# A two-layer encoder on one core: other slots for attention's sums and retention's keys, and one product issued in two pieces

## The chip, the cores and the metric

One core of a Trainium2 chip runs the whole program. The metric is the device time of one execution in microseconds (us). TensorE (PE) multiplies, VectorE (DVE), ScalarE (ACT) and GpSimd (POOL) work on elements, and SyncE (SP) issues nearly all transfers from one queue.

## The reference

Two sequences of 512 tokens, `x_prompt` and `x_sample`, go through the same two layers of width 1024. Below they are the two groups `g`. Each layer adds its mixer's output to `x`, after a norm of the rows of `x`; a last norm ends it. Both mixers have 8 heads, 256 wide.

```python
# layer 0: attention as a difference of two softmaxes per head
q, k, v, gate = split(h @ w_in)                  # 1024 -> 8192
p = softmax(rotary(q) @ rotary(k).T)             # 16 maps of 512 x 512, two per head
a = p[:, :, 0] - lam * p[:, :, 1]
o = rms_norm(a @ v) * silu(gate);  x = x + o @ w_out
# layer 1: retention in both directions
q, k, v, gate = split(h @ w_in)                  # 1024 -> 6144
scores = (q @ k.T) * intra;   o = scores @ v + (q * q_decay) @ state
state  = state * chunk_decay + (k * k_decay).T @ v
o = rms_norm(o_fwd + o_bwd) * silu(gate);  x = x + o @ w_out
```

## The kernel before

**Numbers in two parts.** Every matmul operand is kept as a high part and the rest that is left (`hi_of` on ACT, `lo_of` on DVE, both in fp32r). A product takes three matmuls, high by high, high by low, low by high (`PASSES`), which add up in one PSUM bank.

**Projections.** Both groups are projected together, with a scheme of seven products in place of eight. A `Unit` covers 256 output columns; its products are P1, P2, P5, P6, P3, P7 and P4 (`SEQ`). Each takes one operand made of weights, which lies in a ring of seven work buffers (`ws`), and four tiles made of activations: B11 in slots 0 to 3 (read by P1), B21 in 4 to 7 (P2), T1 in 8 to 11 (P5), T2 in 12 to 15 (P6), B22 in 16 to 19 (P3), T3 in 20 to 23 (P7), T4 in 24 to 27 (P4). A "pair" unit's product is 12 matmuls of 128x512 (`pair`, line 633; queries, keys and gates). A "wide" unit's is 48 of 128x256 (`wide`, line 643; the values): there the activations are stationary and the weights move. `product` issues a product, `evac` what follows it: P7's result is read from a bank (`sums`, line 687) to which P4 then adds. `projections` is a generator that yields after each product, so that the caller can lay other work between two of them. The P4 of a unit comes after the first product of the next; the last unit ends with P3, the P4 of the unit before it, P7, P4.

**Slots.** Most tiles lie in one arena, 18 x 1024 + 128 words of 4 bytes per partition, in slots 1024 words apart (slots 12, 13 and those from 20 on are tiles of their own; 14 to 19 follow 11 in the arena). A tile may be shifted by some words, and then reaches into the next slot's first words:

```python
lo = at * 1024 + shift
...
b.also = Buf(plan, f"edge{at + 1 if shift else at}", 1, None)
```

`edge` lets the plan know of it: a shifted tile must wait for the readers of the next slot too. Behind the arena lie the seven `ws` buffers of 1024 + 32 words with pads of 32 between them; values units use them from word 28 on.

**Heads of attention.** A step `i` of the loop is one tile of 128 queries of one head and group (64 steps). `scores` (line 1186) makes both maps' scores, 3 matmuls of 128x512 each; `row_max`, `exps` and `combine` make the difference of softmaxes; `transp` (line 1231) turns it; its high and low parts go to `aT`, slots 4 and 5, for two tiles together. `av` (line 1251) then multiplies: 24 matmuls of 128x256 for two tiles, values stationary, `aT` moving. `weighed` and `out_step` (lines 858 and 934) do the norm and the output projection. The last four products of the projections are laid between the first steps, one each in steps 0 to 3. Queries lie in slots 0 to 3 and keys in 6 to 9 (both unshifted), values in 10, 11, 14 and 15 shifted by 36.

**Heads of retention.** A block is one head of one group, done in two halves: `state2` (line 1409: keys turned, in slots 6 and 7 shifted by 36, times values, in 0 to 3 unshifted), `score2` (line 1385: keys stationary, queries moving, slots 4 and 5 shifted by 28), `av2` (line 1429: sums of the own half, values stationary and `aT` moving at a shift of 92; line 1437: those of the other half, queries moving). Blocks' tiles are loaded ahead by `fetch2`.

**Order.** Nothing is issued as it is written. All steps are recorded in a `Plan` with an estimated cost, what they read and what they write. `arrange` then plays them through with these estimates and writes out a fixed order for every engine and for SP's queue. PE's steps are taken in the order recorded, save that one that isn't ready lets up to 24 others pass. A product is one step to the plan, while on the chip a tile's next writer waits for the matmuls that read that tile.

Of the kernel before, what the change touches and what calls it, by code (L numbers as in the profile page):

```python
# [10 lines left out]
F32R = mybir.dt.float32r  # L11
# [4 lines left out]
P = 128  # L16
S = 512
D = 1024
KT = D // P
NT = S // P  # L20
# [235 lines left out]
def trunk_kernel(  # L256
# [8 lines left out]
    xs = (x_prompt, x_sample)  # L265
# [116 lines left out]
    def step(gen, n=1):  # L382
        for _ in range(n):
            next(gen, None)
# [24 lines left out]
    def pe(cost, fn, r, w, wait=0.0):  # L409
        plan.op("PE", cost, fn, r, w, wait=wait)  # L410
# [134 lines left out]
    class Unit:  # L545
# [71 lines left out]
            if op == "P2" and self.early is not None:  # L617
                self.early, self.x = None, {}

        def product(self, op):  # L620
            which = BANK_OF[op]
            n_banks = 2 if self.wide else 1
            opens = op in OPENS
            if opens:
                self.banks[which] = [bank(self.tags[which], which) for _ in range(n_banks)]
            a, b = self.ops.pop(op), B_OF[op]
            bt = [Bop[b, k] for k in range(4)]
            reads = [q[1] for q in a] + bt

            def pair(ps, ks=range(4)):  # L630
                for k in ks:
                    for i, (u, v) in enumerate(PASSES):
                        nc.tensor.matmul(  # L633
                            ps.t, a[u][0]()[:, k, :], bt[k][:, v, :], start=(opens and k == 0 and i == 0),
                            stop=(k == 3 and i == 2), skip_group_check=True)

            def wide(ps, t):
                if self.led and op == "P1" and t == 0:
                    for j in range(NT):
                        nc.tensor.transpose(ps[:, j * P:(j + 1) * P], ident.t, ident.t)  # L640
                for k in range(4):
                    for i, (u, v) in enumerate(PASSES):
                        nc.tensor.matmul(  # L643
                            ps[:, (t % 2) * 256:(t % 2) * 256 + 256], bt[k][:, v, t * P:(t + 1) * P],
                            a[u][0]()[:, k, :], start=(opens and t % 2 == 0 and k == 0 and i == 0),
                            stop=(k == 3 and i == 2), skip_group_check=True)

            if not self.wide:
                ps = self.banks[which][0]
                if op == "P1" and self in first_units[:2]:  # L650
                    def piece(k, half):
                        here = slice(half * 256, half * 256 + 256)
                        for i, (u, v) in enumerate(PASSES):
                            nc.tensor.matmul(
                                ps[:, here], a[u][0]()[:, k, :], bt[k][:, v, here], start=(half + k + i == 0),
                                stop=(k == 3 and i == 2), skip_group_check=True)
                    for half in range(2):
                        for k in range(4):
                            pe(0.36, lambda k=k, half=half: piece(k, half),
                               ([(a[0][1][0], (n, k)) for n in range(2)] if self is first_units[0] else reads[:2])  # L660
                               + [(bt[k], (0, half)), (bt[k], (1, half))], [(ps, (k, half))])
                else:
                    pe(2.79, lambda: pair(ps), reads, [ps])
                return
            for t in range(NT):
                ps = self.banks[which][t // 2]
                led = self.led and op == "P1" and t == 0
                pe(1.87 if led else 1.43, lambda ps=ps, t=t: wide(ps, t), reads + [ident] * led, [ps])
# [152 lines left out]
    def projections(units, early):  # L821

        n = 2 + len(early)
        for u, place in zip(units[2:], early):
            u.early = place
        order = product_order(units, n)
        ready = 0
        for n, (u, op) in enumerate(order):
            while ready < len(order):
                v, p = order[ready]  # L830
                if sum(w.n_ws for w, _ in order[n:ready]) + v.n_ws > WS_BUFS:
                    break
                v.prep(p)
                ready += 1
            u.product(op)
            u.evac(op)
            yield

# [33 lines left out]
    def load_qk(src, i, shift):  # L872
        t = slot(i, [P, 2, S], F32R, shift)
        dma(lambda: t.t.bitcast(F32), lambda: src[0][src[1]], [src[0]], [t], 512)
        return t
# [95 lines left out]
    qk_d = {}  # L971
# [194 lines left out]
    def fetch1(h, g, v=True):  # L1166
        for j in range(2):
            for which in range(2):
                qk[h, g, j, which] = load_qk((qk_d[0, which, h, g], j), 6 * which + 2 * g + j, 0)
        if v:  # L1170
            fetch1_v(h, g)

    def fetch1_v(h, g):
        vt[h, g] = load_v(v_d[0, h, g], 10 + 4 * g, 36)
        sg[h, g] = load_sg(g_d[0, h, g])

    def scores(i):
# [47 lines left out]
    def transp(i):  # L1225
        p, n = st[i]['p'], i % 2
        tp = bank("tp", "tpa")

        def fn():
            for j in range(NT):  # L1230
                nc.tensor.transpose(tp[:, j * P:(j + 1) * P], p[:, 0, j * P:(j + 1) * P], ident.t)  # L1231
        pe(0.44, fn, [p, ident], [tp])
        if n == 0:
            st[i]['aT'] = [slot(4 + u, [P, NT, 256]) for u in range(2)]
        aT, here = st[i - n]['aT'], slice(n * P, (n + 1) * P)
        src = lambda: tp.t.rearrange("p (j n) -> p j n", j=NT)
        hi_of(S, lambda: aT[0][:, :, here], src, [tp], [(aT[0], n)])
        lo_of(S, lambda: aT[1][:, :, here], src, lambda: aT[0][:, :, here], [tp, (aT[0], n)], [(aT[1], n)])
# [54 lines left out]
    for i in range(N + 5):  # L1293
        if i % 2 and i > 2:
            fill(1, LAG)
            at(av, i - 3, N)
        at(scores, i, N)
        at(row_max, i, N)
        at(exps, i, N)
        at(combine, i, N)  # L1300
        for n, when in enumerate((0, 1, 2, 3)):
            if i == when:
                step(proj, 1)
                if n >= 2:
                    new_xN(n - 2, lambda t, n=n: (xs[n - 2][0, t * P:(t + 1) * P, :], []))
                if n == 3:
                    fetch1_v(0, 1)
        if not i % 2 or i < 3:
            fill(1, LAG)
        at(transp, i - 1, N)  # L1310
        fill(1, LAG)
        if i % 2 == 0 and i > 3:
            at(weighed, i - 4, N)
        if i < N and i % 4 == 2 and i > 4:
            nh, ng = tiles[i][0:2]
            if ng == 1 and nh + 1 < NH:
                fetch1(nh + 1, 0)
            elif ng == 0 and nh > 0:
                fetch1(nh, 1)
# [24 lines left out]
    def fetch2(b):  # L1344
        h, g = blocks[b]
        for which in range(2):
            qk[b, which] = load_qk((qk_d[1, which, h - h % 2, g], h % 2), (4, 14)[which] + b % 2, (28, 128)[which])
        keys = len(plan.ops) - 1
        vt[b] = load_v(v_d[1, h, g], 2 * (b % 2), 0)
        t = kts[b] = slot(6 + b % 2, [P, 2, S], F32R, 36)  # L1350
        dma(lambda: t.t.bitcast(F32), lambda: kt_d[h, g].rearrange("a p c -> p a c"), [kt_d[h, g]], [t], 512)
        sg[b] = load_sg(g_d[1, h, g])
        return keys
# [22 lines left out]
    def score2(b, c):  # L1376

        h, g = blocks[b]
        s = bank("sc", "s2")
        q, k = qk[b, 0], qk[b, 1]  # L1380

        def fn():
            for j in range(2):
                for i, (u, v) in enumerate(PASSES):
                    nc.tensor.matmul(  # L1385
                        s[:, j * 256:(j + 1) * 256], k[:, u, (2 * c + j) * P:(2 * c + j + 1) * P],
                        q[:, v, c * 256:(c + 1) * 256], start=(j == 0 and i == 0), stop=(i == 2),
                        skip_group_check=True)
        pe(0.71, fn, [q, k], [s])
        t1 = e_t("rt")  # L1390
        F = Fs[h]
        dve(S, lambda: nc.vector.tensor_tensor(
            t1.t, s.t, F[:, 0:4, :].rearrange("p a b -> p (a b)"), op=ALU.mult),
            [s, *((F, n) for n in range(4))], [t1])
        aT = slot(8 + 2 * (b % 2) + c, [P, 2, S], F32R, 92)
        hi_of(S, lambda: aT[:, 0, :], lambda: t1.t, [t1], [(aT, 0)])
        lo_of(S, lambda: aT[:, 1, :], lambda: t1.t, lambda: aT[:, 0, :], [t1, (aT, 0)], [(aT, 1)])
        aTs[b, c] = aT
# [205 lines left out]
```

## Time and profile before

| | us |
|---|---|
| median of three runs (1807.0 to 1808.09) | 1807.33 |
| the profiled execution | 1806.59 |
| span of its instructions | 1804.5 |
| projections of layer 0, from the first to the last full stretch | 48 to 622 |
| attention, with the last four products at its start | 622 to 1010 |
| projections of layer 1 | 1055 to 1490 |
| retention | 1490 to 1804.5 |

Times within the execution are counted from the span's start. "PE o L1251 x24" in the chain of waits means 24 matmuls of line 1251 into a tile named `o`; L415, L419 and L422 are the helpers that record every transfer, high part and low part. In the busy time by stage, engines' columns hold busy us with the count of instructions, then TensorE's granted clock as a share of full speed, the mean busy share of the DMA engines, and GB/s.

### The profile page before, as it was taken

To read this page: it belongs to the slowest core of one execution; us is meant where nothing else is said; L and a number is where in the kernel's file an instruction comes from. 1 tells how busy PE (TensorE), PEld (TensorE's weight loads), DVE (VectorE), ACT (ScalarE), POOL (GpSimd) and SP (SyncE) were. 2 spreads that over 40 slices of the span, in tenths; PEclk is the share of its full clock that TensorE was granted. 3 is DMA by queue.
4 is the path that set the end of the run, shared out by engine and by line. 5 is a ranking of instruction groups with operands and counts; after the bars stand their busy time and mean duration, and the time that the engine had idled before them with its cause. 6 is when DMAs were issued, how large, how long until landed. Compare 5 with 4: busy or idle time off the path is not lost.

```text
span 1804.5 us, 27874 instructions
## 1 busy us (share of the span) xinstructions
PE 1789.8 (99%) x10333; PEld 1566.1 (87%) x10333; DVE 1479.1 (82%) x2344; ACT 895.9 (50%) x1865; POOL 169.2 (9%) x315
## 2 busy tenths in 40 slices
PE   9999999999999999999999999999999999999998
PEld 7889889898988888888888888898989998888887
DVE  8967878778699888888888897787887967888887
ACT  8753344443343565555454866444444455444446
POOL 1000000000000022322322200000000000111113
PEclk9999999999999999999999999999999999999999
DMA  6444455655545594444554524464647459664652
GB/s 218 134 134 135 158 150 166 199 164 155 177 124 187 204 344 179 172 162 156 179 205 140 195 68 147 140 210 156 207 151 231 144 182 399 262 232 185 228 216 94
DMA packets 162767, 328.81 MB, mean 182 GB/s; under 512 B 12724, under 2 KB 76872, under 8 KB 162632
## 3 DMA queue, kind: packets, MB, share of 16 engines
q1 hardware_dynamic: 162160, 326.18, 53.5%
q8 instruction: 81, 1.33, 0.3%
q10 hardware_dynamic: 472, 0.86, 0.1%
q14 instruction: 54, 0.44, 0.1%
HBM read 209.55 MB, written 117.44 MB: 181 GB/s over the span
## 4 chain that ended last, share of the span: by engine, by line
PE 93%; DVE 3%; ACT 1%; DMA 1%; issue 0%; POOL 0%; SPq 0%; ACTq 0%; POOLq 0%; DVEq 0%
PE pj L633 20%; PE pj L934 19%; PE sc L633 11%; PE pj L643 10%; PE o L633 8%; PE o L1251 5%; PE sc L643 5%; PE sc L1186 5%; PE o L1429 2%; PE o L643 2%; PE tp L1231 1%; PE sc L1385 1%; PE tp L1409 1%; PE o L1437 1%; DVE ws L422 1%; DMA raw<-in_da_w_out_dram 1%
## 5 line engine op out<-in xcount | busy, mean ns | idle before, releaser
L934 PE MATMUL pj<-ws,arena 128*128 128x512 f32 x1542 | 389.8, 396 | 0.0
L934 PEld LDWEIGHTS pj<-ws,arena 128*128 128x128 f32 x1542 | 277.3, 188 | 50.6
L633 PE MATMUL pj<-b,ws 128*128 128x512 f32 x1080 | 263.2, 390 | 0.0
L633 PEld LDWEIGHTS pj<-b,ws 128*128 128x128 f32 x1080 | 201.3, 188 | 41.7 <-DVE e L687 0.5
L939 DVE SCALAR_TENSOR_TENSOR b<-pj,pad,b 128x512 f32<-128x512 f32 (+1 forms) x257 | 190.2, 744 | 23.0 <-PE pj L934 21.7
L422 DVE TENSOR_TENSOR ws<-st,ws 128x512 fp32r<-128x512 f32 (+1 forms) x192 | 147.9, 774 | 70.4 <-ACT ws L419 52.8
L422 DVE TENSOR_TENSOR ws<-raw,ws 128x512 fp32r<-128x512 f32 (+2 forms) x167 | 141.9, 855 | 69.4 <-ACT ws L419 59.5
L419 ACT CAST ws<-st 128x512 fp32r<-128x512 f32 (+1 forms) x192 | 132.0, 693 | 123.4 <-PE pj L633 34.6
L633 PE MATMUL sc<-arena,ws 128*128 128x512 f32 x768 | 185.2, 390 | 0.0
L633 PE MATMUL o<-arena,ws 128*128 128x512 f32 x744 | 178.4, 391 | 1.1 <-DVE arena L482 1.1
L633 PEld LDWEIGHTS sc<-arena,ws 128*128 128x128 f32 x768 | 143.9, 188 | 29.7
L419 ACT CAST ws<-raw 128x512 fp32r<-128x512 f32 (+2 forms) x167 | 126.2, 762 | 84.7 <-PE o L633 46.6
L633 PEld LDWEIGHTS o<-arena,ws 128*128 128x128 f32 x744 | 138.5, 188 | 30.3 <-DVE arena L482 2.0
L633 PE MATMUL pj<-arena,ws 128*128 128x512 f32 x624 | 153.1, 390 | 0.0
L633 PEld LDWEIGHTS pj<-arena,ws 128*128 128x128 f32 x624 | 116.4, 188 | 23.9
L1204 ACT ACTIVATE b<-sc,pad 128x512 f32<-128x512 f32 x128 | 87.9, 688 | 69.3 <-DVE pad L1194 68.5
L679 ACT COPY c<-pj 128x512 f32<-128x512 f32 x104 | 60.9, 586 | 115.2 <-PE pj L633 62.7
L643 PE MATMUL pj<-ws,b 128*128 128x256 f32 x960 | 116.9, 275 | 0.0
L643 PEld LDWEIGHTS pj<-ws,b 128*128 128x128 f32 x960 | 113.3, 188 | 0.6
L1186 PE MATMUL sc<-arena 128*128 128x512 f32 x384 | 99.6, 393 | 0.0
L1251 PEld LDWEIGHTS o<-arena 128*128 128x128 f32 x768 | 96.1, 189 | 3.3 <-ACT arena L419 0.7
L1251 PE MATMUL o<-arena 128*128 128x256 f32 x768 | 97.1, 284 | 0.5 <-ACT arena L419 0.5
(221 smaller groups left out, 2875.9 us busy)
## 6 DMA issues: line engine op xcount, KB each, us to landing
qk<-os SPq DMA_DIRECT2D x192, 256.0 KB, 3.4
arena<-qk SPq DMA_DIRECT2D x96, 512.0 KB, 5.9
raw<-in_da_w_in_dram SPq DMA_DIRECT2D x64, 512.0 KB, 4.8
v<-os SPq DMA_DIRECT2D x64, 512.0 KB, 3.7
arena<-v SPq DMA_DIRECT2D x64, 512.0 KB, 4.2
raw<-in_ret_w_in_dram SPq DMA_DIRECT2D x48, 512.0 KB, 4.4
os<-g SPq DMA_DIRECT2D x32, 512.0 KB, 8.1
g<-e SPq DMA_DIRECT2D x48, 256.0 KB, 4.6
```

The lines of the kernel that those rows point to most:

```text
L419: act(n, lambda: nc.scalar.copy(dst(), src()), r, w)
L422: dve(n, lambda: nc.vector.tensor_tensor(dst(), src(), hi().bitcast(F32), op=ALU.subtract), r, w)
L633: nc.tensor.matmul(ps.t, a[u][0]()[:, k, :], bt[k][:, v, :], start=(opens and k == 0 and i == 0), stop=(k == 3 and i == 2), skip_group_che ...
L643: nc.tensor.matmul(ps[:, (t % 2) * 256:(t % 2) * 256 + 256], bt[k][:, v, t * P:(t + 1) * P], a[u][0]()[:, k, :], start=(opens and t % 2 == ...
L679: act(S, lambda c=c, ps=ps: nc.scalar.copy(c.t, ps.t), [ps], [c])
L934: nc.tensor.matmul(ps[:, here], o[a][:, e, t * P:(t + 1) * P], u[b][:, e, here], start=(m == 0), stop=(m == 5))
L939: axpy(n, lambda half=half, here=here, ps=ps: nc.vector.scalar_tensor_tensor(half, ps[:, here], rr[:, t % 2:t % 2 + 1], half, op0=ALU.mult ...
L1186: nc.tensor.matmul(s.t, q[:, a, t * P:(t + 1) * P], k[:, b, :], start=(n == 0), stop=(n == 2))
L1204: act(840, lambda j=j, s=s, m=m: nc.scalar.activation(p[:, j, :], s.t, AF.Exp, bias=m.t, accum_out=sm[:, 2 * j + n:2 * j + n + 1]), [s, m] ...
L1231: nc.tensor.transpose(tp[:, j * P:(j + 1) * P], p[:, 0, j * P:(j + 1) * P], ident.t)
L1251: nc.tensor.matmul(o[:, e * 256:(e + 1) * 256], v[b][:, j, e * P:(e + 1) * P], aT[a][:, j, :], start=(n == 0), stop=(n % 12 == 11), skip_g ...
L1429: nc.tensor.matmul(o[:, e * 256:(e + 1) * 256], v_[v][:, 2 * c + j, e * P:(e + 1) * P], a_[:, u, j * 256:(j + 1) * 256], start=(e == 0 and ...
```

## The change

Three things change, with what they bring along:

- In attention, `aT` is shifted by 28 words, the keys by 64 (`64 * which`; queries stay at 0), and the values by 64 where it was 36.
- In retention, the keys go from slots 14 and 15, shifted by 128, to slots 8 and 9, shifted by 64. The sums' tiles, which lay in slots 8 to 11, go to 10, 11, 14 and 15.
- The very last product of the first layer's projections is issued as two steps of six matmuls, with a yield between them; its bank is read after the second. The loop lays five pieces between its steps 0 to 4, and the second group's `x` is asked for in step 4 where it was step 3.

```diff
-        def product(self, op):
+        def product(self, op, part=None):
...
-            a, b = self.ops.pop(op), B_OF[op]
+            a, b = self.ops[op] if part == 0 else self.ops.pop(op), B_OF[op]
...
+                elif part is not None:
+                    ks = range(2 * part, 2 * part + 2)
+                    pe(1.4, lambda: pair(ps, ks), reads[:2] + [bt[k] for k in ks], [ps])
                 else:
                     pe(2.79, lambda: pair(ps), reads, [ps])
...
-            u.product(op)
+            if units is first_units and n == len(order) - 1:
+                u.product(op, 0)
+                yield
+                u.product(op, 1)
+            else:
+                u.product(op)
...
-                qk[h, g, j, which] = load_qk((qk_d[0, which, h, g], j), 6 * which + 2 * g + j, 0)
+                qk[h, g, j, which] = load_qk((qk_d[0, which, h, g], j), 6 * which + 2 * g + j, 64 * which)
...
-        vt[h, g] = load_v(v_d[0, h, g], 10 + 4 * g, 36)
+        vt[h, g] = load_v(v_d[0, h, g], 10 + 4 * g, 64)
...
-            st[i]['aT'] = [slot(4 + u, [P, NT, 256]) for u in range(2)]
+            st[i]['aT'] = [slot(4 + u, [P, NT, 256], F32R, 28) for u in range(2)]
...
-        for n, when in enumerate((0, 1, 2, 3)):
-            if i == when:
-                step(proj, 1)
-                if n >= 2:
-                    new_xN(n - 2, lambda t, n=n: (xs[n - 2][0, t * P:(t + 1) * P, :], []))
-                if n == 3:
-                    fetch1_v(0, 1)
+        if i < 5:
+            step(proj, 1)
+            if i in (2, 4):
+                new_xN(i // 2 - 1, lambda t, g=i // 2 - 1: (xs[g][0, t * P:(t + 1) * P, :], []))
+            if i == 3:
+                fetch1_v(0, 1)
...
-            qk[b, which] = load_qk((qk_d[1, which, h - h % 2, g], h % 2), (4, 14)[which] + b % 2, (28, 128)[which])
+            qk[b, which] = load_qk((qk_d[1, which, h - h % 2, g], h % 2), (4, 8)[which] + b % 2, (28, 64)[which])
...
-        aT = slot(8 + 2 * (b % 2) + c, [P, 2, S], F32R, 92)
+        aT = slot((10, 14)[b % 2] + c, [P, 2, S], F32R, 92)
```

## The prediction

> **What bounds the kernel now.** I read the page first, then busy time by stage, then the chain of waits in order of time; after that the groups by shape, the waits and the SP queue at the two places where a layer's projections give way to its heads.
>
> ```profile
> span 1804.5 us, 27874 instructions
> ```
>
> ```profile
> core 0: us, PE busy (x) PEld busy (x) DVE busy (x) ACT busy (x) POOL busy (x), PEclk, DMA share, GB/s
> 650.00:1010.00 360.00, 360.00 (x2063) 312.88 (x2062) 298.27 (x460) 187.06 (x503) 103.32 (x210) 1.00 0.49 178
> 1490.00:1516.00 26.00, 24.92 (x160) 22.30 (x160) 18.88 (x32) 15.90 (x31) 0.95 (x2) 1.00 1.03 399
> ```
>
> TensorE (PE) is the bound at a full granted clock. In attention (first stage row) it never idles, while VectorE (DVE) is busy 298.27 of 360 us, 83%. So a matmul that gets faster there shortens the run, until DVE's spare 17% is used up, which a gain of 1% does not do. Around the start of retention (second stage row) PE loses 1.08 us of 26, with the DMA engines full.
>
> "Busy" overlaps, so a matmul's true pace is read from the chain, where pieces follow each other without overlap:
>
> ```profile
> 440.33 5.48 PE pj L643 x48
> 445.81 2.75 PE pj L633 x12
> 448.56 5.48 PE o L643 x48
> 454.04 5.44 PE sc L643 x48
> ...
> 637.39 3.02 PE pj L633 x12
> 640.40 2.87 PE o L1251 x24
> 643.27 0.45 PE tp L1231 x4
> ...
> 646.50 3.14 PE o L1251 x24
> 649.64 1.38 PE sc L1186 x6
> ```
>
> ```profile
> L1251 PE MATMUL o<-arena 128*128 128x256 f32 x768 | 97.1, 284 | 0.5 <-ACT arena L419 0.5
> ...
> L643 PE MATMUL o<-ws,arena 128*128 128x256 f32 x384 | 45.1, 276 | 0.0
> ```
>
> Same engine, same shape (128x256, single column blocks, output in the same kind of bank): the values products (L643) take 5.44/48 = 113 ns each, the attention sums (L1251) 2.87/24 = 120 ns. The first 48 after a run of 512-column products take 5.48 instead of 5.44: a start that costs 0.04 us, and then the pace settles. L1251 starts anew 768/24 = 32 times.
>
> **Part 1: the places of the attention sums.** Counted in words and modulo 64 (slots lie 1024 apart, work buffers 1088 = 17 x 64 apart, and the arena is 290 x 64 long), the values products read their moving operand at 28 and their stationary one at 0; the attention sums read theirs at 0 and 36. The change puts them at 28 and 64, which is 28 and 0. Is it the place that makes 113? Retention has the same contrast:
>
> ```profile
> 1501.21 0.70 PE tp L1409 x6
> 1501.91 0.71 PE sc L1385 x6
> 1502.62 1.38 PE o L1429 x12
> 1504.00 0.68 PE o L1437 x6
> ```
>
> Its sums (L1429) read at 92 = 28 and 0: 12 in 1.38 us with the start included (115 ns), and the 6 of L1437 behind them, moving operand also at 28, take 113. Its state products (L1409) stand at 0 and 36, as attention does: 117, but only 6 long. So three lines agree with the place, and no row shows 0 and 36 settling. I take the pace of L643: 24 x 5.44/48 + 0.04 = 2.76 us a block for 2.87, 0.11 x 32 = 3.5 us. Leaving a settled block also costs: the 12 products behind one take 2.75 (at 445.81) where 12 in mid-stream take 2.72 (a settled run of 12, quoted in part 2), 0.03; the 6 scores behind an attention block take 1.38 where half of 2.72 is 1.36, 0.02 already paid. 0.01 x 32 = 0.3. **Net gain 3.2 us**; ends: 0 (place has no part in it) and 32 x (2.87 - 2.72) = 4.8 (no start cost). Nothing hides this: it is PE's own time on the chain.
>
> The Trainium skill, in the page SBUF — State Buffer, section "Who interferes with whom", speaks against this part: it gives PE two independent read ports, one for the moving operand and one for weights, and has PE wait for no one, so that addresses should not matter and this term would be 0. The trace does not quite agree: 113 and 120 ns stand side by side for one shape.
>
> Writing the sums at word 28 costs ACT and DVE nothing that a row shows: DVE's low halves into attention's slots (place 0) and retention's (place 28) take 684 and 682 ns.
>
> ```profile
> L422 DVE TENSOR_TENSOR arena<-tp,arena 128x512 fp32r<-128x512 f32 x64 | 43.8, 684 | 5.1 <-ACT arena L419 5.0
> ...
> L422 DVE TENSOR_TENSOR arena<-e,arena 128x512 fp32r<-128x512 f32 x36 | 24.4, 682 | 1.2 <-ACT arena L419 1.1
> ```
>
> The scores' keys go from 0 to 64, the same modulo 64: I take 0 for L1186. Its 384 products bound the error: by the nearest contrast of two paces at this width, 2.75 against 2.72 for 12, 0.0025 x 384 = 1 us either way.
>
> **Part 2: retention's keys in slots 8 and 9.** The chain at the start of retention:
>
> ```profile
> 1484.78 2.72 PE sc L633 x12
> 1487.50 2.73 PE pj L633 x12
> 1490.24 0.02 issue
> 1490.25 7.16 DMA arena<-qk
> ```
>
> ```profile
> PE sc L1385 <- DMA arena<-qk: 1.1, 1, 1.1
> ```
>
> The first score (L1385) waits for its keys, until 1490.25 + 7.16 = 1497.4. They go into slot 14 at +128, reaching into slot 15, which T2 holds until P6 ends; P6 is the 12 products from 1487.50, and the load leaves 0.02 after the end. In slots 8/9 at +64 it needs T1's first tiles, read by P5, which ends at 1487.50: up to 2.73 us earlier. With the same 7.16 it lands near 1494.7, while PE has work until 1497.4 - 1.1 = 1496.3. So **the 1.1 us go**, with 1.6 to spare. On SP the load passes two values loads and stores of the gate; the DMA engines are full there (1.03), and what it passes lands up to 0.5 MB / 399 GB/s = 1.3 us later. Nothing else in the stretch stops PE, so I take -1.1, with -1.2 and +0.2 (the wait merely changes its name) as ends. The sums' slots (10, 11, 14, 15 for 8 to 11) are filled by ACT when needed, after P5 and P6; no cost. Places modulo 64 stay, so no pace changes.
>
> **Part 3: the last product in two pieces, and attention's first keys.** The last P4 (12 matmuls, 2.72 settled) now comes as two sixes, one behind the scores of tile 3, one behind those of tile 4. It adds no matmul. From 637.39 to 646.50 PE's work is 2.72 + 2.87 + 0.45 + 1.38 (six scores) + 0.45 (four more transposes) + 0.22 (two more, half of four) = 8.1 of 9.1 us: 1.0 is lost, to these waits:
>
> ```profile
> PEld o L1251 <- ACT arena L419: 0.7, 1, 0.7
> ...
> PEld tp L1231 <- DVE arena L422: 0.5, 1, 0.5
> PEld pj L633 <- DVE e L687: 0.5, 1, 0.5
> ```
>
> The first six still wait for L687 (the sum of P7 reads the bank that P4 adds to). The sums of tiles 0 and 1 then start up to 1.4 us earlier, and the second six fill the wait for the transposes' bank. ACT's and DVE's chain to the next sums is late next. Against it stands a new wait: at +64 the second map's keys of head 0 (slot 7) reach into slot 8, T1 again, so their load waits for P5 where it waited for P2. PE order and SP order are both written out from the planner's estimates, which count P5 as a whole.
>
> ```profile
> 612.60 5.08 SPq L415 DMA_DIRECT2D arena<-qk  x4
> 620.08 0.32 SPq L415 DMA_DIRECT2D arena<-v  x1
> 620.45 0.90 SPq L415 DMA_DIRECT2D arena<-qk  x2
> ```
>
> ```profile
> DMA to landing us min/median/max: 3.2/5.5/10.1
> ```
>
> ```profile
> 622.61 1.52 PE L1186 MATMUL sc<-arena 128*128 128x512 f32 x6
> 623.97 2.88 PE L633 MATMUL o<-arena,ws 128*128 128x512 f32 x12
> ```
>
> Loads that P5 frees leave from 620.08. From there the keys land at 620.1 + 5.5 = 625.6, where the second scores of tile 0 ran at 622.61 + 0.68 = 623.3: 2.3 us late. P3 (2.72) can stand ahead of them and covers that; the tiles behind run some 2 us later, with four products of filler. I take -0.4 for the part; ends -1.0 (all of the lost time) and +2.3 (nothing covers the keys). Behind the waiting load on SP stand the other loads, the values and the second group's keys, which only later tiles read.
>
> **Sum.** The profiled execution took 1806.59 us (span 1804.5 and 2.1 around it), 0.74 below the median 1807.33. -3.2 - 1.1 - 0.4 = -4.7: 1801.9 for such an execution, **1802.6** beside the median. Two runs of this kernel are told apart from about 0.2%, 3.6 us.
>
> **Rivals.**
> A, *the place does nothing* and 120 is due to the order of reads within the block (the attention sums change their stationary tile per key block): for it, no row has the same instructions at two places; against it, L1429 has the same order at the other place and gets 115 with its start. Then -1.1 - 0.4 = -1.5: 1805.8. The port rule of the Trainium skill named above, in SBUF — State Buffer, would give this time.
> B, *another transfer takes the keys' place* in retention, since the engines move 399 GB/s there: for it, the share of 1.03; against it, the 1.6 to spare. Then -3.2 - 0.4 = -3.6: 1803.7.
> C, *attention's first scores wait*: the load of slot 7 leaves at 620.9, with the last of the three that P5 frees now, and takes the longest landing of the window, 10.1: 631.0 for 623.3, 7.7 us late. If P3 is not put ahead, all of it falls on PE: 7.7 + 0.4 - 4.7 = +3.4, 1810.7; with P3 ahead 5.0, +0.7, 1808.0. It ends slower than before once the scores start over 4.3 us late. For it: one SP queue, served in order, and landings of up to 10.1; against it: in the rows above four loads were taken one by one as tiles came free within a product, so this one could leave at about 618 (slot 8 is the first that P5 reads).
> D, *a new order elsewhere*: the planner lays the whole program out anew, and a misplaced step costs what the one at 1490 did, about 1 us each. The sum then lands 1 to 3 us higher, 1803.6 to 1805.6.
>
> **How the numbers follow.** Forecast 0.62, A 0.12, B 0.09, C 0.08, D 0.09. The forecast's own bounds, 32 blocks at 0.08 to 0.13 us and part 3 at -1.0 to +0.6, give 1801 to 1804. The range takes in B, A and most of D: 1800.8 to 1806.2, leaving C and odd ends out. Faster by over 0.2% means below 1803.7: 0.55 of the forecast's 0.62, half of B, a little of D: 0.62. Within 0.2%: the rest of these, A, and most of C: 0.31. Slower: 0.07, from C's far end and from what I don't see.
>
> **What would show it.** Right: in the chain, blocks of L1251 x24 at 2.74 to 2.78; its mean near 276 ns; no wait of L1385 for DMA, and the first score of retention 1 us or more closer to the product ahead of it; the stretch from the last P7 to the sums of tiles 2 and 3 shorter by some 0.4. Wrong: L1251 still at 2.87 (A); PE waiting for another transfer before 1516 (B); L1186 <- DMA arena<-qk at the start of attention (C). An L1186 slower per three would say that 64 is not 0 for the chip.

## The result and the profile after

The changed kernel takes 1802.00 us, the median of 7 runs (1801.44 to 1802.73); the kernel before, run beside it, 1807.36 (7 runs, 1806.56 to 1808.30). The ratio is 0.997 with an interval of 0.9961 to 0.998: faster by 5.4 us, and by more than what two runs of this kernel need to be told apart. The forecast was 1802.6, or 4.7 us less. The profiled execution took 1801.96 us (1806.59 before), with this span:

```profile
span 1799.9 us, 27878 instructions
```

Busy time by stage of the changed kernel, in the two stretches shown of before (engines' busy us with counts, TensorE's granted clock, DMA share, GB/s):

```profile
650.00:1010.00 360.00, 360.00 (x2087) 312.86 (x2087) 299.84 (x462) 190.15 (x508) 106.36 (x210) 1.00 0.50 181
1490.00:1516.00 26.00, 25.16 (x166) 22.52 (x165) 21.75 (x38) 14.98 (x34) 1.90 (x4) 1.00 1.04 411
```

Attention is still PE from end to end, at a full clock, and now gets 2087 matmuls done where 360 us held 2063. At the start of retention PE still loses 26 - 25.16 = 0.84 us, with the DMA engines as full as before. The chain of waits of the changed kernel at the start of attention (start, us, what):

```profile
620.17 2.72 PE pj L633 x12
622.89 0.68 PE sc L1194 x3
623.57 2.72 PE o L633 x12
626.29 1.36 PE sc L1194 x6
...
636.07 0.70 PE sc L1194 x3
636.77 1.37 PE pj L633 x6
638.14 0.68 PE sc L1194 x3
638.82 2.76 PE o L1259 x24
641.58 0.44 PE tp L1239 x4
642.02 1.39 PE sc L1194 x6
643.40 1.38 PE pj L633 x6
644.79 0.44 PE tp L1239 x4
645.23 0.24 PE o L866 x2
645.47 0.69 PE sc L1194 x3
646.16 1.39 PE pj L942 x6
647.55 2.77 PE o L1259 x24
```

A block of sums (L1259, which was L1251) takes 2.76 us instead of 2.87, and each row starts where the one before ends: the 1.0 us of waits that stood here before is gone. The two halves of the last P4 are the two "pj L633 x6". The first scores come as threes with P3 (623.57) between the first and second map, so P3 did go ahead of the late keys. The group of the sums on the page:

```profile
L1259 PE MATMUL o<-arena 128*128 128x256 f32 x768 | 93.7, 277 | 0.0
```

Where the time came from is read by following the same steps through both timelines of PE. First the kernel before (start, us, engine, line, operation, tiles, count, and in brackets the idle time and what ended it):

```profile
622.61 1.52 PE L1186 MATMUL sc<-arena 128*128 128x512 f32 x6
...
1009.31 3.03 PE L1251 MATMUL o<-arena 128*128 128x256 f32 x24
...
1492.78 0.86 PE L1409 MATMUL tp<-arena 128*128 128x256 f32 x6
...
1497.45 0.98 PE L1385 MATMUL sc<-arena 128*128 128x256 f32 x6 [1.08 <-DMA arena<-qk]
...
1515.90 0.38 PE L858 MATMUL tp<-ident,m 128*128 128x128 f32 x2
```

Then the kernel after:

```profile
622.73 0.84 PE L1194 MATMUL sc<-arena 128*128 128x512 f32 x3
...
1004.90 2.92 PE L1259 MATMUL o<-arena 128*128 128x256 f32 x24
...
1488.27 0.86 PE L1416 MATMUL tp<-arena 128*128 128x256 f32 x6
...
1492.30 0.97 PE L1392 MATMUL sc<-arena 128*128 128x256 f32 x6 [0.43 <-DMA arena<-qk]
...
1511.29 0.44 PE L866 MATMUL tp<-ident,m 128*128 128x128 f32 x2 [0.41 <-DVE b L422]
```

The first scores of attention start 0.12 us later than before, the last block of sums 4.41 earlier: attention gave 4.5 (forecast 3.2 + 0.4). Of these the sums gave 3.4: from the start of each of their 768 products to the start of the next they take 91.9 us before and 88.5 after. The other 1.1 are the waits that are gone. Until retention's first state product nothing more comes (4.51 earlier). Its first scores are 5.15 earlier, so the keys gave 0.64; at the transposes of line 866 only 4.61 is left, with a wait for DVE that was not there before: 0.54 was given back. The end is 4.6 earlier.

### The profile page after: what moved, and what is told of

Its sections match the earlier page's. It is cut to its first block, busy times and chain, and to the rows that moved or that the text cites. A ratio compares the mean times of both kernels' runs of the same rounds, so it can differ in the third digit from the quotient of the medians.

```text
span 1799.9 us, 27878 instructions
## 1 busy us (share of the span) xinstructions
PE 1785.8 (99%) x10333; PEld 1563.0 (87%) x10333; DVE 1479.0 (82%) x2344; ACT 896.5 (50%) x1865; POOL 170.1 (9%) x315
## 4 chain that ended last, share of the span: by engine, by line
PE 93%; DVE 3%; DMA 2%; ACT 1%; issue 0%; POOL 0%; ACTq 0%; SPq 0%; POOLq 0%; DVEq 0%
PE pj L633 20%; PE pj L942 19%; PE sc L633 10%; PE pj L643 10%; PE o L633 8%; PE o L1259 5%; PE sc L1194 5%; PE sc L643 5%; PE o L643 2%; PE o L1436 2%; PE tp L1239 2%; PE sc L1392 1%; PE o L1444 1%; PE tp L1416 1%; DMA raw<-in_ret_w_out_dram 1%; DVE ws L422 1%
## 5 line engine op out<-in xcount | busy, mean ns | idle before, releaser
L942 PE MATMUL pj<-ws,arena 128*128 128x512 f32 x1542 | 389.6, 396 | 0.0
L942 PEld LDWEIGHTS pj<-ws,arena 128*128 128x128 f32 x1542 | 277.5, 188 | 50.9
L633 PE MATMUL pj<-b,ws 128*128 128x512 f32 x1080 | 263.3, 390 | 0.0
L633 PEld LDWEIGHTS pj<-b,ws 128*128 128x128 f32 x1080 | 201.3, 188 | 41.3
L633 PE MATMUL sc<-arena,ws 128*128 128x512 f32 x768 | 185.2, 389 | 0.0
L633 PE MATMUL o<-arena,ws 128*128 128x512 f32 x744 | 178.4, 391 | 1.1 <-DVE arena L482 1.1
L633 PEld LDWEIGHTS sc<-arena,ws 128*128 128x128 f32 x768 | 144.0, 188 | 29.8
L633 PEld LDWEIGHTS o<-arena,ws 128*128 128x128 f32 x744 | 138.5, 188 | 30.2 <-DVE arena L482 2.0
L633 PE MATMUL pj<-arena,ws 128*128 128x512 f32 x624 | 153.1, 390 | 0.0
L633 PEld LDWEIGHTS pj<-arena,ws 128*128 128x128 f32 x624 | 116.4, 188 | 23.9
L1194 PE MATMUL sc<-arena 128*128 128x512 f32 x384 | 100.7, 394 | 0.0
L1259 PEld LDWEIGHTS o<-arena 128*128 128x128 f32 x768 | 93.2, 188 | 2.7
L1259 PE MATMUL o<-arena 128*128 128x256 f32 x768 | 93.7, 277 | 0.0
```

The lines of the kernel that those rows point to most:

```text
L633: nc.tensor.matmul(ps.t, a[u][0]()[:, k, :], bt[k][:, v, :], start=(opens and k == 0 and i == 0), stop=(k == 3 and i == 2), skip_group_che ...
L942: nc.tensor.matmul(ps[:, here], o[a][:, e, t * P:(t + 1) * P], u[b][:, e, here], start=(m == 0), stop=(m == 5))
L1194: nc.tensor.matmul(s.t, q[:, a, t * P:(t + 1) * P], k[:, b, :], start=(n == 0), stop=(n == 2))
L1259: nc.tensor.matmul(o[:, e * 256:(e + 1) * 256], v[b][:, j, e * P:(e + 1) * P], aT[a][:, j, :], start=(n == 0), stop=(n % 12 == 11), skip_g ...
```

## The experiments

Each time stands beside the kernel before run on the same chip; "less" is the difference of the two medians.

**Each part of the change alone (e1, e2, e3), and the change without the moving operand's new place (e4).** Edits to the kernel before, then to the changed one:

```diff
 e1_places (before)
-    load_qk((qk_d[0, which, h, g], j), 6 * which + 2 * g + j, 0)
+    load_qk((qk_d[0, which, h, g], j), 6 * which + 2 * g + j, 64 * which)
-    vt[h, g] = load_v(v_d[0, h, g], 10 + 4 * g, 36)
+    vt[h, g] = load_v(v_d[0, h, g], 10 + 4 * g, 64)
-    st[i]['aT'] = [slot(4 + u, [P, NT, 256]) for u in range(2)]
+    st[i]['aT'] = [slot(4 + u, [P, NT, 256], F32R, 28) for u in range(2)]
 e2_ret_slots (before)
-    (4, 14)[which] + b % 2, (28, 128)[which])
+    (4, 8)[which] + b % 2, (28, 64)[which])
-    aT = slot(8 + 2 * (b % 2) + c, [P, 2, S], F32R, 92)
+    aT = slot((10, 14)[b % 2] + c, [P, 2, S], F32R, 92)
 e3_split (before): the last product in two pieces, and the loop's five pieces
 e4_moving_0 (after)
-    st[i]['aT'] = [slot(4 + u, [P, NT, 256], F32R, 28) for u in range(2)]
+    st[i]['aT'] = [slot(4 + u, [P, NT, 256]) for u in range(2)]
```

> The kernel before with attention's places alone: aT at 28, keys at 64, values at 64; last product whole, retention's slots as before. If the place sets the pace, blocks of L1251 take 2.76 us for 2.87 and the time falls by 3.3 to 3.5 us, less up to 2 us if the later load of the first keys shows at the start of attention. If the place does nothing (rival A), L1251 stays at 2.87 and the time within 1 us of before.

> The kernel before with retention's keys in slots 8 and 9 and its sums in 10, 11, 14 and 15, nothing else. My forecast of this term was -1.1 us, all of it the wait of the first score. The trace of the changed kernel says: the wait shrinks by about 0.65 us and about 0.57 comes back some 13 us later, where PE waits for VectorE (norm's transposes, bank freed by L422). By that the time falls by only 0.1 us, up to 0.3.

> The kernel before with the last product of the first projections in two pieces, nothing else (keys stay at 0, so the first keys' load waits for P2 as before). If the split fills the lost time at the start of attention, -0.7 to -1.0 us. If the gain seen there in the changed kernel came from the other order of the first scores, which the shifted keys brought, then near 0.

> The changed kernel with attention's aT back at 0: moving operand at 0, stationary values at 64, which is 0. Same instructions in nearly the same order. If 28 for the moving operand is what lets the pace settle at 113 ns, blocks of L1259 take 2.83 to 2.87 us and the time is 2.5 to 3.5 us above the changed kernel. If it is enough that the values leave 36, blocks stay at 2.76 and the time does too. If the order of reads sets the pace (rival A), no difference either.

| kernel | median us (before: 1807.05) | ratio, interval | less |
|---|---|---|---|
| e1_places | 1803.28 | 0.9979 (0.997 to 0.9988) | 3.77 |
| e2_ret_slots | 1806.68 | 0.9999 (0.999 to 1.0008) | 0.37 |
| e3_split | 1805.84 | 0.9994 (0.9985 to 1.0002) | 1.21 |
| e4_moving_0 | 1805.02 | 0.9989 (0.998 to 0.9998) | 2.03 |

The three parts sum to 5.35, the whole change to 5.36. Each interval reaches some 1.6 us to either side, and those of e2 and e3 hold 1, so by the runs alone only e1 of the three is told apart from before, and that the sums agree this closely is chance. In e4 a single place differs from the changed kernel, and a block of sums is back at its old length in the chain of waits. The traces of the two hold the same instructions in the same order on PE, DVE and ACT, all through the program:

```profile
638.75 2.88 PE o L1259 x24
647.60 2.86 PE o L1259 x24
```

That costs 5.36 - 2.03 = 3.3 us (3.0 by the two medians themselves). Two rows of e4's timeline of PE, the last block of sums and retention's first scores, stand against 1004.90 and 1492.30 in the changed kernel:

```profile
1008.27 3.04 PE L1259 MATMUL o<-arena 128*128 128x256 f32 x24
1495.20 0.88 PE L1392 MATMUL sc<-arena 128*128 128x256 f32 x6
```

By the last block 3.37 are lost, about 32 blocks at 0.11 (3.5); 0.47 come back at the scores, which wait less for their keys. So the place of the moving operand makes the pace. With the values and keys moved and `aT` not, no block is faster; e4's 2.03 is about what the other two parts give (0.37 + 1.21).

The waits of e3, from 620 to 650, with the old places and the product in two pieces:

```profile
PEld pj L633 <- DVE e L690: 0.6, 1, 0.6
PE pj L633 <- DVE e L690: 0.2, 1, 0.2
```

Of the three waits of before only that for the sum of P7 is left. In e1 the chain of waits has blocks of 2.76 to 2.77 from the first on; retention's keys are still waited for there (1.3 us on PE). In e2 that wait is small and a new one stands behind it; from its waits, 1485 to 1518:

```profile
PEld tp L858 <- DVE b L422: 0.5, 1, 0.5
PEld sc L1385 <- DMA arena<-qk: 0.5, 1, 0.5
PE tp L858 <- DVE b L422: 0.3, 1, 0.3
```

**The wait that came back in retention (e6), and the change without its retention part (e9).** If the transposes of line 866 wait for their bank, another bank should free them:

```diff
 e6_rows_in_pj (after)
-    rr = norm_cols(sqs[b, c], bank("tp", "rows"), ...
+    rr = norm_cols(sqs[b, c], bank("pj" if (b, c) == (0, 1) else "tp", "rows"), ...
 e9_no_ret (after): the two lines of e2 back to what they were
```

> The changed kernel with one bank moved: the norm's transposes (L866) of the second half of retention's first block go to a bank of the output products, so that they no longer wait for VectorE to empty the state's bank (L422). If that wait alone gives back what the earlier keys brought, the time falls by 0.4 to 0.6 us below the changed kernel. If VectorE's own backlog at the start of retention is the limit, PE waits 0.4 to 0.6 us somewhere else within the next 10 us, and the time stays within 0.2.

> The changed kernel with retention's slots as before (keys in 14 and 15 at 128, sums in 8 to 11); attention's places and the split stay. If retention's part is worth what its own run showed, 0.4 us, the time is 0.2 to 0.5 above the changed kernel, and the first score waits for its keys again by 1 us or more. By my forecast of that part it would be 1.1 above. If it brings nothing: the same.

e6: 1802.64 beside 1806.89, ratio 0.9977 (0.9968 to 0.9986), 4.25 less. The wait of line 866 is gone, and a longer one stands one step earlier; its timeline of PE:

```profile
1505.92 0.96 PE L1392 MATMUL sc<-arena 128*128 128x256 f32 x6
1507.98 0.98 PE L1416 MATMUL tp<-arena 128*128 128x256 f32 x6 [1.11 <-ACT tp L870]
```

With the other bank the planner also set 26 matmuls of PE, all between 1506 and 1512 us, in another order, so this says only that PE does not get through this stretch sooner by having that bank free in that order. e9: 1802.46 (1802.02 to 1805.23) beside 1807.25, ratio 0.9976 (0.9966 to 0.9986), 4.79 less; the wait for the keys is back, and that for DVE is not there:

```profile
PE sc L1392 <- DMA arena<-qk: 1.6, 1, 1.6
```

The retention part is thus worth 5.36 - 4.79 = 0.6 us on top of the others and 0.37 alone (e2), both within the width of the intervals. The wait for the keys is 1.1 in the kernel before, but 1.3 to 1.7 in e1, e3 and e9, the three with a changed attention and the keys in their old slots; why it is longer there no run tells.

**Other places for the sums (e5, e10, e11).** How far does the place decide? Edits to the changed kernel:

```diff
 e5_both_28:    vt[h, g] = load_v(v_d[0, h, g], 10 + 4 * g, 92)
 e10_moving_32: st[i]['aT'] = [slot(4 + u, [P, NT, 256], F32R, 32) for u in range(2)]
 e11_moving_16: st[i]['aT'] = [slot(4 + u, [P, NT, 256], F32R, 16) for u in range(2)]
```

> The changed kernel with attention's values at 92, so that moving and stationary operand both stand at 28. If the moving operand's place alone decides, blocks of L1259 stay at 2.76 us. If the two must differ as they do in the values products (28 and 0), the blocks go back to 2.83 to 2.87 and the time to about 1805.

> The changed kernel with aT at 32, moving operand at 32, values at 0. If places count modulo 32, it is place 0: blocks of L1259 at 2.87 us. If only 64 counts and any place away from the stationary one will do: 2.76.

> The changed kernel with aT at 16, moving operand at 16, values at 0. If 28 works because it lies at the end of a stretch of 32, 16 gives something between 2.76 and 2.87; if any place off a multiple of 32 will do, 2.76.

One run each. From the chains of waits, a block as it stands at 650 or soon after, in e5, e10 and e11:

```profile
658.92 2.84 PE o L1259 x24
```

```profile
668.63 2.88 PE o L1259 x24
```

```profile
668.68 2.83 PE o L1259 x24
```

| moving, stationary operand at, modulo 64 | kernel | block, us | run, us (before beside it) |
|---|---|---|---|
| 28, 0 | after | 2.76 | 1802.00 (1807.36) |
| 16, 0 | e11 | 2.83 | 1803.73 (1807.25) |
| 28, 28 | e5 | 2.80 to 2.84 | 1803.15 (1806.89) |
| 0, 36 | before | 2.87 | 1807.36 |
| 0, 0 | e4 | 2.86 to 2.88 | 1805.02 (1807.05) |
| 32, 0 | e10 | 2.84 to 2.89 | 1804.82 (1807.25) |

It is both operands' places together: 28 for the moving one helps most beside a stationary one at 0. By the starts of successive matmuls in the trace (medians over the 32 blocks), the changed kernel's products follow at 114 to 120 ns for the first ten of a block and at 113 from there to its end; in e4, at 0 and 0, at 120 from the third to the last; in e5 they repeat 116, 117, 119, 118 and never settle, and in e10 they repeat 118, 120, 122. A shift by itself is not it, since e10 has one too. Nor is the distance between the two operands: counted modulo 64 it is 28 in the kernel before (0, 36) as in the changed one (28, 0). Nor do places count modulo 32 alone: 32 takes as long as 0 here, but not for the wider products below. That 64 is the right stretch to count by was assumed throughout; no run tests it. No run tells which part of the chip asks for this either.

**The same idea for wider products (e7, e8, e12).** If 28 is good for 128x256, is it for the 128x512 products of the output projection (L942) and the scores (L1194), whose operands lie at 0 and 0? Edits to the changed kernel:

```diff
 e7_weights_28
-    hi, lo = ws_t([P, 2, S]), ws_t([P, 2, S])
+    hi, lo = ws_t([P, 2, S], True), ws_t([P, 2, S], True)
 e8_keys_28 (e7, and)
-    ... 6 * which + 2 * g + j, 64 * which)
+    ... 6 * which + 2 * g + j, 92 * which)
-    vt[h, g] = load_v(v_d[0, h, g], 10 + 4 * g, 64)
+    vt[h, g] = load_v(v_d[0, h, g], 10 + 4 * g, 128)
 e12_weights_32: the weights of the output projection at word 32 of their buffer
```

> The changed kernel with the output projection's weights (moving operand of L942, 128x512) at word 28 of their buffers, stationary activations at 128, which is 0. With 512 columns the pace settles at 227 ns at place 0 already; only the start of a run costs, some 26 ns per six. If the place also sets that start, the 256 sixes change by up to 26 ns each, so up to 6 us faster. If the start costs the same at any place: within 0.5 us of the changed kernel.

> As the run with the weights at 28, and attention's keys (moving operand of L1194, 128x512) at 92, which is 28, the values at 128, which is 0. The scores' 128 threes cost 9 ns over their settled pace in the changed kernel. If the place sets the start: up to 1 us faster than with the weights alone; if not: the same within 0.5.

> The changed kernel with the output projection's weights (moving operand of L942, 128x512) at word 32 of their buffers instead of 0. At 28 this product never settled and the run was 3 us longer. If places count modulo 32: the same pace and time as the changed kernel, within 0.3. If not: pace and start differ, and the time by up to 3 us either way.

| kernel | median us (before) | ratio, interval | less |
|---|---|---|---|
| e7_weights_28 | 1805.08 (1806.89) | 0.9989 (0.9981 to 0.9998) | 1.81 |
| e8_keys_28 | 1805.55 (1806.89) | 0.9993 (0.9984 to 1.0002) | 1.34 |
| e12_weights_32 | 1808.18 (1807.25) | 1.0003 (0.9994 to 1.0012) | -0.93 |

The group of line 942 on the pages of the changed kernel, of e7 and of e12:

```profile
L942 PE MATMUL pj<-ws,arena 128*128 128x512 f32 x1542 | 389.6, 396 | 0.0
```

```profile
L942 PE MATMUL pj<-ws,arena 128*128 128x512 f32 x1542 | 391.7, 397 | 0.0
```

```profile
L942 PE MATMUL pj<-ws,arena 128*128 128x512 f32 x1542 | 394.8, 399 | 0.0
```

All three lose against the changed kernel: e7 by 5.36 - 1.81 = 3.5 us (3.1 by the two medians), of which the line's busy time shows 2.1; e12 by 6.3 (6.2), with 5.2 in the line; e8 adds 0.5 to e7's loss, less than the width of the intervals, so nothing shows that 28 helps the scores. The best pair that was tried for 256 columns, 28 and 0, is a worse one for 512 than 0 and 0. None of the twelve kernels beats the changed one.

## Why the prediction came out

**Part 1, the places: right in mechanism and size.** Forecast was 3.2; the sums themselves take 3.4 us less in the trace, in e1 (88.5 for 91.9) as in the changed kernel. By the medians e1 alone gives 3.77 and the step back in e4 costs 3.3. The block of 2.76 is the forecast's own number, and the group's mean went from 284 to 277 ns. "Is it the place that makes 113?" was answered from two lines with the same shape; e4 answers it with the same line, and rival A falls. The rule of the Trainium skill, SBUF — State Buffer, section "Who interferes with whom", by which PE reads the two operands through two independent ports and waits for no one, does not account for this: it speaks of ports and not of addresses, and that addresses should therefore not matter was the prediction's own reading. The changed kernel and e4 differ in one place only, and their blocks take 2.76 and 2.87. The measurement decides: for these products the places count. The new place of the keys (64 for 0) cost the scores nothing that shows: in the chain six take 1.36 us behind a product of the same width (626.29), the settled pace of 12 in 2.72.

**Part 2, retention's keys: the step that failed is "nothing else in the stretch stops PE", and "with the same 7.16" was too short.** Forecast was 1.1, measured 0.37 (e2) to 0.6 (e9). SP's queue in the kernel before, then after:

```profile
1490.25 0.32 SPq L415 DMA_DIRECT2D arena<-qk  x1
...
1493.21 2.30 SPq L415 DMA_DIRECT2D arena<-qk  x2
1495.60 0.39 SPq L415 DMA_DIRECT2D raw<-in_ret_w_out_dram  x1
```

```profile
1482.96 0.39 SPq L415 DMA_DIRECT2D arena<-qk  x1
...
1485.74 2.88 SPq L415 DMA_DIRECT2D arena<-qk  x2
1489.27 2.11 SPq L415 DMA_DIRECT2D g<-e  x2
1492.32 0.38 SPq L415 DMA_DIRECT2D raw<-in_ret_w_out_dram  x1
```

The key load leaves 7.29 us earlier, of which 4.51 came from attention: 2.8, as forecast. But it lands at 1492.25, so it took 9.3 us where 7.16 was assumed: 2.1 more, which uses up the 1.6 to spare and leaves the 0.43 of wait. This is so in every run: in the ten with the keys in slots 8 and 9 this load takes 8.6 to 9.3 us (8.87 in e2's chain), in the four with the old slots 7.2 to 7.8. And the load of the output projection's weights (`raw`) leaves only 3.28 us earlier than before, not 4.5. Two stores of the gate now stand ahead of it, but they are issued by 1491.4; what SP then waits for, from its own waits between 1492 and 1492.4, is this:

```profile
SPq L415 <- DMA arena<-qk: 0.9, 1, 0.9
```

It is the landing of the keys' load itself, and the weights leave 0.07 us behind it. In the ten runs with the new slots they leave 0.06 to 0.07 us after the keys have landed, in the four with the old ones 0.06 to 0.14 after a store of the gate has. So keys that land late hold back the weights too. What follows is in DVE's timeline of the changed kernel:

```profile
1502.24 1.23 DVE L422 TENSOR_TENSOR ws<-raw,ws 128x1024 fp32r<-128x1024 f32 x1 [0.56 <-ACT ws L419]
...
1510.16 0.74 DVE L947 SCALAR_TENSOR_TENSOR b<-pj,pad,b 128x512 f32<-128x512 f32 x1
1510.82 0.41 DVE L422 TENSOR_TENSOR b<-tp,b 128x256 fp32r<-128x256 f32 x1
```

DVE waits 0.56 for the weights and then runs end to end; it empties the transposes' bank at 1510.82, which is 4.47 earlier than before (1515.29), while PE had come 5.15 ahead. PE waits the 0.41. In before, DVE was as full here (11.80 of 12 us from 1504.6), but PE came late enough. Nine traces with the new slots, all but e6, show the same pair (DVE waiting 0.26 to 0.91 for those weights, PE 0.33 to 0.71 for the bank), and the four with the old slots, before, e1, e3 and e9, where PE waits over 1 us for the keys, show neither. So rival B was half right: another transfer and DVE behind it took most of the place. That the weights' load alone decides this is read from these traces; no run moved it by itself.

**Part 3, the split: right in direction, sized too small.** Forecast 0.4 between ends of -1.0 and +2.3, measured 1.21 by the medians of e3, whose interval holds 0 as well. The traces are sharper: e3's span is 0.8 shorter (1803.7 for 1804.5), with 0.2 of the lost 1.0 still there, and in the changed kernel attention gave 1.1 beside the sums, the whole of the lost time. I had charged part of it to "ACT's and DVE's chain to the next sums" and to late keys. Neither came: in the chain of after the next sums start without a wait at 647.55. For rival C, SP's queue shows a load of keys that leaves at 618.37, before the rest of what P5 frees (from 620.20), as the rows in the prediction suggested. It lands at 624.03, and P3 stands ahead of the second scores (626.29). Its far end needed both to fail.

**Rival D**, a new order elsewhere, shows a price at one place at most: SP's queue at the start of retention, where the weights now wait for the keys. Its price there is the 0.54 given back, below the 1 to 3 us set for it.

So the mechanism of part 1, which is most of the sum, was right, but that 4.7 came out so closely was luck, two errors that cancel. From trace to trace the parts gave 3.4, 1.1 (part 3) and 0.64 - 0.54 = 0.1 (part 2), 4.6 in all, where 3.2, 0.4 and 1.1 were forecast. By the medians part 2 is worth 0.4 to 0.6, since e9, the changed kernel without it, waits 1.6 for these keys where the kernel before waits 1.1. All of these differences are smaller than the width of the intervals of the runs.

## What to carry to other kernels

When one engine is the bound from end to end, compare the pace of its like instructions row by row: two lines of one shape at 113 and 120 ns were worth more here than every visible wait, and the place of an operand is a cheap thing to try, one pair for each shape. A wait that is removed on a full engine is worth what the next engine's slack allows: before counting a wait of 1.1 us as gained, look whether the engine that empties PE's banks is itself end to end behind it. Nor does a load that leaves earlier land earlier by as much: here, into full DMA engines, most of the lead was lost.

## What the chip showed that was not expected

- The pace of back-to-back products depends on the places of both operands: for 128x256, 113 ns (28, 0), 117 to 118 (28, 28 and 16, 0), 120 (0, 0; 0, 36; 32, 0), the last in threes of 118, 120, 122.
- The good pace is not there at once: ten products at 114 to 120 come first, by the medians over the 32 blocks.
- What is good for 256 columns is bad for 512: moving the output projection's weights from 0 to 28 costs 3.1 to 3.5 us, to 32 6.2 to 6.3 us, over 1542 products.
- A load of keys sent 2.8 us earlier beside full DMA engines (411 GB/s) took 9.3 us for 7.2, and lost 2.1 of its lead; over all runs it took 7.2 to 7.8 in its old place and 8.6 to 9.3 in the new one.
- The next load of weights left SP's queue 0.06 to 0.07 us after those keys had landed, in all ten runs with the new slots.
